# The entry of a two-layer encoder trunk: scale and shift summed on another engine, in pairs, with the loads and transposes in a new order

## The chip, the cores and the metric

The kernel runs on one core of a Trainium2 chip. The metric is device time in microseconds (us) of one execution, as the median of several runs; beside it stands one execution recorded by the hardware profiler. The engines are TensorE (PE: matrix products and transposes, results in PSUM), VectorE (DVE), ScalarE (ACT), GpSimd (POOL) and SyncE (SP, which issues most loads). Each engine works through its own queue in order.

## The reference, cut to what matters

Two layers over a sequence of 1024 tokens with 1024 features, all in float32. Only the first operation of layer 0 is touched by the change:

```
c_act = silu(c)
mod   = c_act @ ada_w[0] + ada_b[0]                  # 1024 x 6144 weights
sh_m, sc_m, g_m, sh_f, sc_f, g_f = split(mod, 6)
h   = rmsnorm(x, norm_g[0, 0]) * (1 + sc_m) + sh_m
bcx = h @ conv_in_w[0]                               # 1024 x 3072: b_gate, c_gate, xh
y   = (b_gate * short_conv(c_gate * xh)) @ conv_out_w[0]
```

Behind it come the rest of layer 0 (norm, MLP of width 4096), a shared key and value side, and layer 1 with latent attention and a second MLP.

## The kernel before, in words

`conv_phase` (L841) is the entry. The eight tiles of x, 128 tokens each (`xt`), are loaded by `load_x` in two halves of 512 tokens and divided by their root mean square in `norm_x`: ScalarE squares a tile and takes the root (`squares`, L269), VectorE inverts it and scales the tile (L964). The features are cut into eight blocks k of 128 columns. For a block and a half, `turn` transposes four 128x128 pieces on TensorE (L899), and `scaled` applies the block's scale and shift: ScalarE writes the result twice (L905), once rounded to the product format (`hi`) and once in full, and VectorE writes the remainder (`lo`, L906). `products` (L924) then multiplies the block with one column group of conv_in_w: three gates, three matmuls each for hi and lo parts, nine matmuls of 512 columns for a block and a half. The weights of a block are loaded and split into the same two parts by `weights` (L913; ScalarE L160, VectorE L161).

The scale and shift of a block come from 2 x 128 columns of `ada_w` with 1024 rows. `ada` loads them (four loads of 256 KB into one of three buffers `aw`), and `ada_end` (L884) multiplies the eight row groups with silu(c), kept in `csil`, and accumulates on VectorE (L887, L889); two float32 matmuls with a column of ones (L891) sum over the partitions, and VectorE adds gain and bias into `sh[k]` (L892, L894).

The loop of L986 goes over k; the second half of x follows the first two blocks behind (`LAG`). The output column group m=0 is finished here; for m=1 the same operands are multiplied again (L1009 on), while VectorE forms the sums that the later groups need (`sums`, L948). `pinned` fixes the order of an engine's queue as written: in this stretch of TensorE and SP; ScalarE and VectorE are ordered by the scheduler of the framework. The gains and biases are loaded as rows on ScalarE's queue at the start (L130 to L139), transposed on TensorE (L864, L867) and copied by VectorE.

Of the kernel before, what the change touches and what calls it, by code (L numbers as in the profile page):

```python
# [36 lines left out]
LAG = 2  # L37
# [12 lines left out]
def trunk_kernel(ctx: ExitStack, tc: tile.TileContext, x, c, ada_w, ada_b, norm_g, conv_in_w, conv_w,  # L50
# [73 lines left out]
    nc.scalar.activation(csil, craw, AF.Exp, scale=-1.0)  # L124
# [3 lines left out]
    vrows, brows = rows_[:, :P], rows_[:, P:2 * P]  # L128
    r = 0
# [8 lines left out]
    nc.scalar.dma_start(brows[0:96, :], ada_b.rearrange("l (k p) -> (l k) p", p=P))  # L138
    nc.scalar.dma_start(brows[96:112, :], kv_ada_b.rearrange("(k p) -> k p", p=P))  # L139
# [23 lines left out]

    nc.vector.tensor_scalar(csil, csil, 1.0, None, op0=ALU.add)
# [676 lines left out]
    def conv_phase():  # L841
# [20 lines left out]

        p_ = tp_ps()
        nc.tensor.transpose(p_[:, :VEC_ROWS], vrows[:VEC_ROWS, :], ident[:VEC_ROWS, :VEC_ROWS])  # L864
        nc.vector.tensor_copy(vecs, p_[:, :VEC_ROWS])
        p_ = tp_ps()
        nc.tensor.transpose(p_[:, :BIAS_ROWS], brows[:BIAS_ROWS, :], ident[:BIAS_ROWS, :BIAS_ROWS])  # L867
        nc.vector.tensor_copy(bias, p_[:, :BIAS_ROWS])
# [15 lines left out]
        def ada_end(k, raw):  # L884
            p_ = tp_ps()
            acc = st.tile([P, 2 * P], F32, tag="av", name=nm("av"), bufs=2)
            nc.vector.tensor_scalar(acc, raw[:, 0, :], csil[:, 0:1], None, op0=ALU.mult)  # L887
            for i in range(1, KD):
                nc.vector.scalar_tensor_tensor(acc, raw[:, i, :], csil[:, i:i + 1], acc, op0=ALU.mult, op1=ALU.add)  # L889
            for j in range(2):  # L890
                nc.tensor.matmul(p_[:, j:j + 1], acc[:, j * P:(j + 1) * P], ones[:, 0:1], start=True, stop=True)  # L891
# [21 lines left out]
        def weights(k, m):  # L913
# [3 lines left out]
               conv_in_w[0][k * P:(k + 1) * P, :].rearrange("p (g c) -> p g c", g=3)[:, :, m * P:(m + 1) * P])  # L917
# [48 lines left out]
        def first_half(k):  # L966
# [4 lines left out]
            elif k == LAG:  # L971
                load_x(1)
# [9 lines left out]
        with pinned([mybir.EngineType.PE, mybir.EngineType.SP]):  # L982
# [3 lines left out]
            for k in range(KD + LAG):  # L986
# [12 lines left out]
                if k == KD:  # L999
                    w.append(weights(0, 1))  # L1000
# [530 lines left out]
```

## Time and profile before

| | |
|---|---|
| median of 3 runs | 2171.38 us (2169.84 to 2172.59) |
| profiled execution | 2170.84 us, span of its records 2169.1 us |
| TensorE busy | 2068.5 us, 95% of the span |
| VectorE, ScalarE busy | 1542.0 us, 1083.7 us |
| mean granted TensorE clock | 0.988 |

The span is the time from the first to the last recorded instruction. Busy times of engines overlap. A granted clock of 1.00 is 2.4 GHz, 0.50 is 1.2 GHz. Times in rows count from the start of the span.

### The profile page before, as it was taken

Reading aid. Unit: us, or ns where it says so; the run is one execution under the profiler, and the core shown is the slowest. Engines: PE = TensorE matmul, PEld = TensorE weight load, DVE = VectorE, ACT = ScalarE, POOL = GpSimd, SP = SyncE. Lnnn points to the kernel's source line nnn. Section 1 sums busy time; section 2 is a strip of 40 time slices with the busy share of each in tenths; the row PEclk is TensorE's granted clock in tenths of the full one; section 3 lists DMA queues with packets and bytes.
Section 4 is the critical chain, followed back from the end, with each engine's and each line's share of the span. In section 5 each row is a group of like instructions: output and inputs, shape, how many; then the busy total and the mean of one; then the engine's idle time right before and its main releaser. Section 6 shows DMA issues by size and latency. Waiting matters only on the chain.

```text
span 2169.1 us, 25064 instructions
## 1 busy us (share of the span) xinstructions
PE 2068.5 (95%) x9438; PEld 1690.3 (78%) x9438; DVE 1542.0 (71%) x2087; ACT 1083.7 (50%) x1533; POOL 5.3 (0%) x13
## 2 busy tenths in 40 slices
PE   4999999889999999998999999989899999999998
PEld 3788878678888788886777888878678888788886
DVE  6877866877655669877688887665876665566576
ACT  4533353735554444455665655564744454544443
POOL 0000000000000000000000000000000000000000
PEclk9999999999999999998999999999999999999999
DMA  7344464256444889546213331043255553774355
GB/s 227 112 140 146 137 200 143 85 195 206 152 146 141 285 289 327 191 152 216 87 50 123 94 104 36 29 156 127 77 194 185 189 170 121 268 247 164 96 174 172
DMA packets 251023, 344.47 MB, mean 159 GB/s; under 512 B 19253, under 2 KB 142482, under 8 KB 250902
## 3 DMA queue, kind: packets, MB, share of 16 engines
q1 hardware_dynamic: 208408, 252.50, 37.0%
q10 hardware_dynamic: 42494, 90.38, 11.2%
q8 instruction: 74, 1.21, 0.2%
q14 instruction: 47, 0.39, 0.1%
HBM read 258.94 MB, written 83.89 MB: 158 GB/s over the span
## 4 chain that ended last, share of the span: by engine, by line
PE 75%; DVE 13%; ACT 6%; DMA 4%; issue 2%; ACTq 0%; SPq 0%; DVEq 0%
PE one L157 41%; PE mm L157 19%; PE tp L157 7%; PE big L157 4%; PE big L1334 2%; ACT junk L272 2%; DMA raw<-in_ada_w_dram 1%; DVE y L328 1%; PE tp L1360 1%; DVE raw L329 1%; DVE acc L187 1%; DMA raw<-ha 1%; DVE av L889 1%; ACT z L1192 1%; DMA aw<-in_ada_w_dram 1%
## 5 line engine op out<-in xcount | busy, mean ns | idle before, releaser
L157 PE MATMUL one<-slot,uphi 128*128 128x512 f32 x1224 | 377.8, 390 | 0.0
L157 PEld LDWEIGHTS one<-slot,uphi 128*128 128x128 f32 x1224 | 230.4, 188 | 48.1 <-issue 0.5
L157 PE MATMUL one<-ring,ring 128*128 128x512 f32 x1152 | 263.0, 390 | 2.3 <-DVE ring L161 2.3
L157 PEld LDWEIGHTS one<-ring,ring 128*128 128x128 f32 x1152 | 215.8, 188 | 48.4 <-ACT ring L160 3.1
L157 PE MATMUL one<-slot,uplo 128*128 128x512 f32 x612 | 240.9, 394 | 8.6 <-DVE y L516 3.8
L161 DVE TENSOR_TENSOR uplo<-raw,uphi 128x1024 fp32r<-128x1024 f32 x127 | 153.2, 1221 | 131.2 <-ACT uphi L160 131.2
L161 DVE TENSOR_TENSOR ring<-raw,ring 128x1024 fp32r<-128x1024 f32 x144 | 174.2, 1219 | 55.8 <-ACT ring L160 55.4
L160 ACT ACTIVATE ring<-raw 128x1024 fp32r<-128x1024 f32 x144 | 149.5, 1051 | 110.6 <-DMA raw<-ha 60.2
L157 PE MATMUL mm<-ring,ring 128*128 128x512 f32 x768 | 189.3, 396 | 7.0 <-DVE ring L161 7.0
L160 ACT ACTIVATE uphi<-raw 128x1024 fp32r<-128x1024 f32 x127 | 134.5, 1060 | 113.0 <-PE one L157 82.1
L157 PE MATMUL big<-slot 128*128 128x512 f32 x768 | 178.9, 393 | 5.3 <-DVE slot L161 4.5
L157 PE MATMUL tp<-ring,ring 128*128 128x512 f32 x768 | 183.9, 389 | 0.0
L160 ACT ACTIVATE ring<-w 128x1024 fp32r<-128x1024 f32 x80 | 84.8, 1060 | 186.0 <-PE tp L157 95.7
L157 PEld LDWEIGHTS mm<-ring,ring 128*128 128x128 f32 x768 | 146.3, 191 | 39.8 <-DVE ring L161 6.0
L157 PEld LDWEIGHTS big<-slot 128*128 128x128 f32 x768 | 144.5, 189 | 36.5 <-DVE slot L161 5.2
L157 PEld LDWEIGHTS tp<-ring,ring 128*128 128x128 f32 x768 | 144.0, 188 | 29.8
L161 DVE TENSOR_TENSOR ring<-w,ring 128x1024 fp32r<-128x1024 f32 x80 | 97.7, 1221 | 88.5 <-ACT ring L160 87.9
L157 PEld LDWEIGHTS one<-slot,uplo 128*128 128x128 f32 x612 | 115.3, 188 | 36.8 <-DVE y L516 5.5
L187 DVE SCALAR_TENSOR_TENSOR acc<-raw,csil,acc 128x1024 f32<-128x1024 f32 x88 | 112.5, 1279 | 27.6 <-DMA raw<-in_ada_w_dram 23.1
L514 ACT ACTIVATE y<-one 128x512 f32<-128x512 f32 x66 | 39.0, 592 | 165.0 <-PE one L157 111.3
L157 PE MATMUL mm<-slot,uphi 128*128 128x512 f32 x344 | 108.7, 398 | 9.5 <-DVE slot L386 9.3
L157 PE MATMUL one<-slot,s 128*128 128x512 f32 x468 | 114.5, 394 | 3.3 <-DVE s L161 3.3
(268 smaller groups left out, 3464.9 us busy)
## 6 DMA issues: line engine op xcount, KB each, us to landing
ha<-y ACTq DMA_DIRECT2D x224, 256.0 KB, 4.1
raw<-ha SPq DMA_DIRECT2D x112, 512.0 KB, 4.0
raw<-in_ada_w_dram SPq DMA_DIRECT2D x80, 512.0 KB, 4.0
raw<-in_mlp_up_w_dram SPq DMA_DIRECT2D x70, 512.0 KB, 4.2
w<-in_mlp_down_w_dram SPq DMA_DIRECT2D x48, 512.0 KB, 6.8
raw<-in_mlp_down_w_dram SPq DMA_DIRECT2D x32, 512.0 KB, 4.7
raw<-in_conv_in_w_dram SPq DMA_DIRECT2D x18, 512.0 KB, 4.0
xs<-raw ACTq DMA_DIRECT2D x18, 512.0 KB, 2.6
```

Of the source, the lines that this page charges most:

```text
L157: nc.tensor.matmul(out_, lhs[a], rhs[b], start=first and i == 0, stop=last and i == 2, skip_group_check=more)
L160: nc.scalar.activation(hi, src, AF.Copy)
L161: nc.vector.tensor_tensor(lo, src, hi.bitcast(F32), op=ALU.subtract)
L187: nc.vector.scalar_tensor_tensor(acc, raw, s, acc, op0=ALU.mult, op1=ALU.add)
L272: nc.scalar.activation(junk, src, AF.Square, accum_out=ss)
L328: nc.vector.scalar_tensor_tensor(y, y, rroot(ss), self.gmb, op0=ALU.mult, op1=ALU.mult)
L329: nc.vector.tensor_tensor(xr, xr, y, op=ALU.add)
L514: nc.scalar.activation(dst, x_, AF.Copy)
L889: nc.vector.scalar_tensor_tensor(acc, raw[:, i, :], csil[:, i:i + 1], acc, op0=ALU.mult, op1=ALU.add)
L1192: nc.scalar.activation(y[32 * i:32 * i + 32, :], p_[32 * j:32 * j + 32, :], AF.Copy, scale=scale)
L1334: nc.tensor.matmul(o_, a, m_, start=j == 0, stop=j == 4)
L1360: nc.tensor.transpose(p_[:, c:c + P], pts[4 * hf + i][:, j * P:(j + 1) * P], ident)
```

## The change

Scale and shift of blocks 0 and 1 are summed wholly on TensorE: 16 matmuls with the weights as the stationary operand and a column of `csil` as the moving one (`ada_one`). Blocks 2 to 7 are taken in pairs: one load buffer of twice the width (`aw2`, three of them), one accumulation on VectorE over 512 columns for two blocks (`ada_sum`), and the sums over partitions as before (`ada_two`). The first half of x is loaded ahead of everything else on SP's queue, and the loads of all blocks are issued in one row. In the loop the transposes and the scaling of a block and half stand one step ahead of the products, and two steps of the next pair's accumulation are written into each step. The order of ScalarE and VectorE is fixed as written as well. On ScalarE's queue the bias rows are loaded ahead of the other vectors, and two small activations (`warm`) call for the function tables of Exp and Sqrt.

```diff
     ld(craw, c.rearrange("o (k p) -> p (o k)", p=P))
-    nc.scalar.activation(csil, craw, AF.Exp, scale=-1.0)
     nc.scalar.dma_start(cs, consts[:, :C_T])
...
+    nc.scalar.dma_start(brows[0:96, :], ada_b.rearrange("l (k p) -> (l k) p", p=P))
+    nc.scalar.dma_start(brows[96:112, :], kv_ada_b.rearrange("(k p) -> k p", p=P))
...
+    warm = small()
+    nc.scalar.activation(warm, eps_1, AF.Exp)
+    nc.scalar.activation(csil, craw, AF.Exp, scale=-1.0)
+    nc.scalar.activation(warm, eps_1, AF.Sqrt)
...
+        load_x(0)
...
-        def ada(k):
+        def ada(k, n=1):
-            raw = st.tile([P, KD, 2 * P], F32, tag="aw", name=nm("aw"), bufs=3)
+            raw = st.tile([P, KD, 2, n * P], F32, tag=f"aw{n}", name=nm("aw"), bufs=2 if n == 1 else 3)
             for i in (0, 4):
                 for j, col in enumerate((D, 0)):
-                    ld(raw[:, i:i + 4, j * P:(j + 1) * P],
-                       w0[i * P:(i + 4) * P, col + k * P:col + (k + 1) * P].rearrange("(k p) m -> p k m", p=P))
+                    ld(raw[:, i:i + 4, j, :],
+                       w0[i * P:(i + 4) * P, col + k * P:col + (k + n) * P].rearrange("(k p) m -> p k m", p=P))
...
+        def ada_one(k, raw):
+            p_ = tp_ps()
+            for j in range(2):
+                for i in range(KD):
+                    nc.tensor.matmul(p_[:, j:j + 1], raw[:, i, j, :], csil[:, i:i + 1], start=i == 0, stop=i == KD - 1)
+            ada_end(k, p_)
+
+        def ada_sum(raw):
+            acc = st.tile([P, 2, 2 * P], F32, tag="av", name=nm("av"), bufs=2)
+
+            def step(i):
+                if i == 0:
+                    nc.vector.tensor_scalar(acc, raw[:, 0], csil[:, 0:1], None, op0=ALU.mult)
+                else:
+                    nc.vector.scalar_tensor_tensor(acc, raw[:, i], csil[:, i:i + 1], acc, op0=ALU.mult, op1=ALU.add)
+
+            return acc, [lambda i=i: step(i) for i in range(KD)]
+
+        def ada_two(k, acc):
+            for i in range(2):
+                p_ = tp_ps()
+                for j in range(2):
+                    nc.tensor.matmul(p_[:, j:j + 1], acc[:, j, i * P:(i + 1) * P], ones[:, 0:1], start=True, stop=True)
+                ada_end(k + i, p_)
...
         with pinned([mybir.EngineType.PE, mybir.EngineType.SP]):
...
+            raws, ws = [ada(0)], [load_weights(0, 0)]
+            load_x(1)
+            raws.append(ada(1))
+            ws.append(load_weights(1, 0))
+            raws += [ada(k, 2) for k in (2, 4, 6)]
             acc = banks6()
...
+            with pinned([mybir.EngineType.Activation, mybir.EngineType.DVE]):
+                norm_x(0)
+                w.append(split_weights(ws[0]))
+                ada_one(0, raws[0])
+                scaled(0, turn(0, 0), *place(0, 0))
+                products(w[0], 0, 0, acc)
+                norm_x(1)
+                w.append(split_weights(ws[1]))
+                ada_one(1, raws[1])
+                scaled(1, turn(1, 0), *place(1, 0))
+                scaled(0, turn(0, 1), *place(0, 1))
+                products(w[1], 1, 0, acc)
+                scaled(1, turn(1, 1), *place(1, 1))
+                products(w[0], 0, 1, acc)
+                av, steps = ada_sum(raws[2])
+                for step in steps:
+                    step()
+                ws = [load_weights(k, 0) for k in (2, 3)]
+                before = 1, 1
+                for k in range(2, KD, 2):
+                    w += [split_weights(q) for q in ws]
+                    ada_two(k, av)
+                    more = k + 2 < KD
+                    if more:
+                        av, steps = ada_sum(raws[k // 2 + 2])
+                    ws = [load_weights(k + i, 0) for i in (2, 3)] if more else [load_weights(0, 1)]
+                    for i in range(k, k + 2):
+                        for half in range(2):
+                            scaled(i, turn(i, half), *place(i, half))
+                            if more:
+                                steps.pop(0)()
+                                steps.pop(0)()
+                            products(w[before[0]], *before, acc)
+                            before = i, half
+                products(w[before[0]], *before, acc)
+            w = split_weights(ws[0])
```

## Rows read from the trace of the kernel before

**Rows 1.** Stretches: us, busy PE, PEld, DVE, ACT, POOL, clock, DMA share, GB/s

```profile
0.00:86.35 86.35, 54.95 (x243) 42.97 (x244) 57.82 (x142) 45.25 (x77) 1.48 (x9) 0.94 0.62 176
...
86.35:119.00 32.65, 32.65 (x146) 27.03 (x145) 28.73 (x43) 15.60 (x27) 0.96 (x1) 1.00 0.58 178
```

**Rows 2.** Chain that ended last, in order of time: start, us, what

```profile
29.09 4.85 DMA aw<-in_ada_w_dram
...
84.37 2.13 PE one L157 x8
```

**Rows 3.** Groups of VectorE, 0 to 86.35 us: busy us, mean ns, idle before

```profile
L889 DVE SCALAR_TENSOR_TENSOR av<-aw,csil,av 128x256 f32<-128x256 f32 x56 | 26.6, 481 | 1.4 <-DMA aw<-in_ada_w_dram 0.5
L161 DVE TENSOR_TENSOR w<-w,w 128x384 fp32r<-128x384 f32 x11 | 6.1, 553 | 1.8 <-ACT w L160 1.8
L964 DVE TENSOR_SCALAR y<-y,small 128x1024 f32<-128x1024 f32 x8 | 6.0, 750 | 0.1
...
L892 DVE SCALAR_TENSOR_TENSOR sh<-tp,g,b 128x1 f32<-128x1 f32 x8 | 1.7, 217 | 5.0 <-PE tp L891 5.0
```

**Rows 4.** One line later in the kernel (L1183): duration min/median/max in ns

```profile
L1183 DVE SCALAR_TENSOR_TENSOR lat<-lat,vecs,sq x8: 737/744/752, 1075.3 to 1131.2; 128x512 f32<-128x512 f32 x8
```

**Rows 5.** Timeline of TensorE: start, us, instruction, what it waited for

```profile
39.84 0.99 PE L891 MATMUL tp<-ones,av 128*128 128x1 f32 x4 [6.90 <-DVE av L889]
40.69 2.91 PE L157 MATMUL mm<-slot,w 128*128 128x512 f32 x6
...
62.22 0.58 PE L891 MATMUL tp<-ones,av 128*128 128x1 f32 x4 [0.39 <-DVE av L889]
62.65 1.63 PE L157 MATMUL mm<-slot,w 128*128 128x512 f32 x6
...
78.56 0.60 PE L899 MATMUL tp<-cs,y 128*128 128x128 f32 x4
...
81.08 0.60 PE L899 MATMUL tp<-cs,y 128*128 128x128 f32 x4
```

**Rows 6.** Stretches, as rows 1, for the loads

```profile
0.00:9.50 9.50, 0.00 (x0) 0.00 (x0) 2.74 (x11) 2.01 (x3) 1.48 (x9) 1.00 0.78 209
10.50:13.50 3.00, 0.83 (x2) 0.36 (x2) 1.56 (x7) 2.88 (x5) 0.00 (x0) 1.00 1.01 385
...
28.50:34.50 6.00, 4.44 (x23) 3.55 (x21) 3.70 (x12) 4.92 (x10) 0.00 (x0) 1.00 1.21 291
```

**Rows 7.** Stretches, as rows 1, for the clock

```profile
36.50:43.50 7.00, 3.66 (x11) 3.11 (x12) 6.05 (x16) 1.45 (x2) 0.00 (x0) 0.51 0.56 152
...
45.50:48.00 2.50, 0.88 (x3) 0.52 (x4) 2.43 (x6) 2.07 (x4) 0.00 (x0) 1.00 0.00 0
68.50:70.00 1.50, 0.20 (x2) 0.23 (x3) 1.50 (x4) 0.04 (x1) 0.00 (x0) 1.00 0.00 0
71.00:74.00 3.00, 3.00 (x9) 2.22 (x9) 0.69 (x1) 1.25 (x2) 0.00 (x0) 0.50 0.23 66
```

**Rows 8.** Timeline of the start: start, us, instruction

```profile
6.75 0.32 ACTq L139 DMA_DIRECT2D raw<-in_kv_ada_b_dram  x1
...
10.59 1.06 ACT L272 ACTIVATE junk<-y 128x1024 bf16<-128x1024 f32 x1 [2.94 <-DMA y<-in_x_dram]
...
12.23 0.42 PE L867 MATMUL tp<-cs,raw 112*128 112x112 f32 x1 [0.92 <-DMA raw<-in_kv_ada_b_dram]
...
13.25 1.04 ACT L272 ACTIVATE junk<-y 128x1024 bf16<-128x1024 f32 x1
...
14.62 1.04 ACT L272 ACTIVATE junk<-y 128x1024 bf16<-128x1024 f32 x1
```

**Rows 9.** Groups of ScalarE, 0 to 86.35 us, as rows 3

```profile
L905 ACT ACTIVATE slot<-tp,sh 128x512 fp32r<-128x512 f32 x12 | 9.3, 778 | 23.4 <-DVE sh L894 19.4 <-PE tp L899 2.9 <-DVE small L279 1.0
...
L160 ACT ACTIVATE w<-w 128x384 fp32r<-128x384 f32 x11 | 5.7, 520 | 7.5 <-PE one L157 2.8 <-DMA w<-in_conv_in_w_dram 2.1 <-DMA aw<-in_ada_w_dram 1.9
...
L124 ACT ACT_TABLE_LOAD x1 | 1.3, 1283 | 3.7 <-DMA cs<-in_consts_dram 3.7
```

More of the change, by code (lines that the diff above doesn't have):

```diff
@@ L36 @@
 AHEAD = 4
-LAG = 2
 PAIRS = D_FF // P // 2
@@ L861, in load_x @@
                 ld(xt[t], x0[t * P:(t + 1) * P, :])
+        load_x(0)
+        p_ = tp_ps()
+        nc.tensor.transpose(p_[:, :BIAS_ROWS], brows[:BIAS_ROWS, :], ident[:BIAS_ROWS, :BIAS_ROWS])
+        nc.vector.tensor_copy(bias, p_[:, :BIAS_ROWS])
         p_ = tp_ps()
@@ L873, in conv_phase, with ada_end @@
         sh = [cp.tile([P, 2], F32, name=nm("sh")) for _ in range(KD)]
-        def ada(k):
-            raw = st.tile([P, KD, 2 * P], F32, tag="aw", name=nm("aw"), bufs=3)
+        def ada(k, n=1):
+            raw = st.tile([P, KD, 2, n * P], F32, tag=f"aw{n}", name=nm("aw"), bufs=2 if n == 1 else 3)
             for i in (0, 4):
                 for j, col in enumerate((D, 0)):
-                    ld(raw[:, i:i + 4, j * P:(j + 1) * P],
-                       w0[i * P:(i + 4) * P, col + k * P:col + (k + 1) * P].rearrange("(k p) m -> p k m", p=P))
-            return raw
[L884 to L891, printed above, removed]
+                    ld(raw[:, i:i + 4, j, :],
+                       w0[i * P:(i + 4) * P, col + k * P:col + (k + n) * P].rearrange("(k p) m -> p k m", p=P))
+            return raw
+        def ada_end(k, p_):
             nc.vector.scalar_tensor_tensor(sh[k][:, 0:1], p_[:, 0:1], g1[:, k:k + 1], b1[:, k:k + 1], op0=ALU.mult,
@@ L911, in conv_phase, with load_weights @@
         new = [None] * 4
-        def weights(k, m):
+        def load_weights(k, m):
             raw = ad.tile([P, D], F32, tag=("acc", "gmb")[k % 2], name=nm("w"), bufs=1)[:, :3 * P]
@@ L920, in weights @@
             return w
+        def weights(k, m):
+            return split_weights(load_weights(k, m))
         late = []
@@ L964, in norm_x, with place @@
                 nc.vector.tensor_scalar(xt[t], xt[t], rroot(squares(nx, xt[t])), None, op0=ALU.mult)
-        def first_half(k):
-            raw = ada(k)
-            if k == 0:
-                load_x(0)
-                norm_x(0)
-            elif k == LAG:
-                load_x(1)
-            p_ = turn(k, 0)
-            ada_end(k, raw)
-            scaled(k, p_, old(k), ("11", "21")[k // 4])
-        def second_half(k):
+        def place(k, half):
+            if not half:
+                return old(k), ("11", "21")[k // 4]
@@ L978, in second_half @@
             if k < 4:
                 new[k] = halves(raw_tile())
-            scaled(k, turn(k, 1), new[k % 4][k // 4], ("12", "22")[k // 4])
+            return new[k % 4][k // 4], ("12", "22")[k // 4]
         with pinned([mybir.EngineType.PE, mybir.EngineType.SP]):
-            w = [weights(0, 0)]
-            first_half(0)
-            acc = banks6()
-            for k in range(KD + LAG):
-                if k < KD - 1:
-                    w.append(weights(k + 1, 0))
-                    first_half(k + 1)
-                if k < KD:
-                    products(w[k], k, 0, acc)
-                if k == LAG:
-                    norm_x(1)
-                    second_half(0)
-                if k >= LAG:
-                    if k - LAG < KD - 1:
-                        second_half(k - LAG + 1)
-                    products(w[k - LAG], k - LAG, 1, acc)
-                if k == KD:
-                    w.append(weights(0, 1))
```

10 lines of the change are left out of this document (4 added, 6 removed).

## Prediction

> **What bounds the kernel now.** I read three views for the first 119 us, the only part that the change touches: the stretches, the chain that ended last, and the timeline. The stretches [rows 1] show two regimes. Up to 86.35 us the matrix engine (TensorE, PE) is busy 55.0 us of 86.35 and starved for the rest; from there it is busy 32.65 of 32.65 us. The boundary is the end of the products of block column m=0: the chain puts the last eight of them at 84.37 to 86.5 us [rows 2], and the 144 products of m=1 then run without a pause, 0.227 us each [rows 1]. What follows is set by TensorE, so a microsecond gained or lost before 86.35 should reach the end nearly whole. In the starved part the chain alternates between VectorE's accumulation (`ada_end`) and loads of the modulation weights that are issued late because their three buffers are still in use; one such row stands for three [rows 2]. So I need one number: E, the time at which the products of m=0 end in the changed kernel, against 86.35.
>
> **What is removed.** Eight accumulations leave VectorE: each seven instructions of 0.481 us plus a first one [rows 3], about 3.8 us, 30 us in all. In come three accumulations over pairs, eight instructions of 512 elements each. The nearest row of that shape took 0.744 us [rows 4]; with a hand-over of 0.04 us, an estimate, I take 0.78, so 6.2 us a pair and 18.7 in all. Blocks 0 and 1 go to TensorE: 16 calls with one column each. The trace records four instructions for two such calls, 0.43 us at the full clock (62.22 to 62.65) and 0.85 us from 39.84 to 40.69, when the granted clock was 0.50, the 1.2 GHz level [rows 5, 7]. A block is 32 instructions: 3.4 us or 6.8 us. VectorE saves 11 us, but that is worth something only where it is what TensorE waits for, so I follow the new order.
>
> **Term 1, the load queue.** All loads of the entry are now issued in one go on SP's queue, in this order: half of x (2.10 MB), block 0 and its product weights (1.05 + 0.20), the other half of x (2.10), block 1 with its weights (1.25), three pairs (6.29), and only then the product weights of blocks 2 and 3 (0.39). No buffer wait holds any of it. Rates: rows of x in 4 KB pieces moved at 385 GB/s, modulation weights in 512 B pieces at 290 [rows 6]. From a start at about 2.2 us (at these rates the 1.99 MB of the first 9.5 us [rows 6] take some 7): x with 0.19 MB of small vectors 6.0, to 8.2; block 0 4.3, to 12.5; x 5.4, to 17.9; block 1 4.3, to 22.2. The pairs come in 1 KB pieces, which no row shows: between 16.3 us (385) and 21.7 us (290). A cost per piece plus one per byte fitted through the two rows puts 1 KB near 345 GB/s, an estimate; I take 18.2 us, to 40.4. Blocks 2 and 3's product weights add 1.4, to 41.8. Those 1.99 MB end just past the first x tile (the 1.95th MB), whose reader started at 10.59 [rows 8]: 1.1 us to land. So the last of them is there at **42.9**, bounds 41.0 and 46.4.
>
> The Trainium skill ("DMA: Bandwidth & Descriptors", Specifications) states that pieces of 512 B and more reach the line rate. By it the wider pieces of a pair gain nothing over single ones. By it the weights land at 46.4, by the fit at 42.9. The trace disagrees with it for single pieces, 290 against 385 GB/s [rows 6]; no row shows the doubled ones.
>
> On VectorE the splits of these two weights stand ahead of `ada_end`, so blocks 2 and 3 wait for them: ScalarE's copy 0.52, VectorE's remainder 0.55, then 0.22 for the scale and about as much for the shift [rows 3, 9]; with hand-overs 1.5 us. The transposes of block 2 start at **G = 44.4** by this path.
>
> **Term 2, the engines' own path to G.** ScalarE's queue: its nine loads ended at 7.07 with 1.5 us of table load and Exp between them [rows 8, 9], so 5.6 without; then two table loads of 1.28 and three small instructions, 8.9. The table loads now precede x instead of following it, which is the saving of `warm`. Four squares at a pitch of 1.37 (13.25 to 14.62 [rows 8]) and the last scaling 0.75 [rows 3]: half of x is ready at 15.5. TensorE meanwhile sums block 0 from about 11.5 (the last small vector, issued 1.5 us earlier than in the kernel before, was transposed there at 12.23 [rows 8]; the loads of block 0 land by 13.6) to between 16.5 and 18.3. Scaling, then ScalarE turns to the other half of x (5.5 us): 26 to 27. Block 1's sums on TensorE stand behind the products of block 0 and end between 25.5 (full clock) and 31 (half). Then two halves scaled (four passes of 0.78 [rows 9], which overlap to some 0.68 each), the remainders, products, the last transposes of block 1 and its remainder: 34 to 38. Only then, in VectorE's fixed order, the pair sum of blocks 2 and 3: 6.2. Then 1.1 for the splits and 0.4: G = 41.7 to 46. Both paths end close together; the queue's 44.4 is the middle, and I take it. It means TensorE stands idle from about 34 to 44 except for 0.8 us of sums, where the kernel before had 6.9 us of idle time at 33 to 40 and then ran until 43.5 at clock 0.50, 3.7 us [rows 5, 7]. I charge the same here: 1.9 us.
>
> **Term 3, after G.** A step is four transposes and nine products: 78.56 to 81.08, 2.52 us [rows 5]. Twelve steps, 30.2; the last nine products 2.04. VectorE needs about 0.7 for the remainder (also 512 elements from two operands, as in [rows 4]) and 1.56 for two sum steps per step, 2.3 against 2.52, so within a pair TensorE sets the pace and "a step ahead" hides ScalarE's passes. At the two borders between pairs it does not: from the start of a pair's last transposes, 0.6 for them, 1.35 for ScalarE's two passes, 0.7 and 1.56 on VectorE, then TensorE's eight one-column instructions, the splits ahead of `ada_end` (1.1) and `ada_end`: 5.65 us until the next transposes, where a step alone is 2.52. So 3.1 more per border, 6.2 for two, of which some 2.3 each are idle time of TensorE. Sum: 30.2 + 2.0 + 6.2 + 1.9 = 40.4, E = 84.8. Idle stretches of that length cost the clock in one case (after 68.4 to 70.2 the clock was 0.50 from 71 to 74) and not in another (45.6 to 48) [rows 7]. With two of them I charge one drop, half of just over 3 us, 1.6: **E = 86.4**, +0.1 us; bounds none and 3.2.
>
> **Smaller parts.** Bias and vector loads change places on ScalarE's queue, covered by the x loads; uncovered it would be a microsecond at the start, and the start has 2 us of slack against the queue. Product weights from block 4 on wait for the splits two blocks back and then have a whole pair, 13 us, to land. The sums of m=1 can no longer begin early (5 us of VectorE work moved behind E): VectorE was busy 28.7 of 32.65 us there, part of it filler needed much later [rows 1]; I take nothing.
>
> **Rivals.**
> *Faster.* The pairs move as x does. Then the weights land at 41.0 and G is 42.5 at a start in full clock; TensorE's idle stretch shrinks and the clock survives it and the borders: 42.5 + 38.5 = 81.0, -5.3 us, **2165.5**. For it: the pieces are twice as long and x reached 385. Against it: the engines' own path must run at its quick end too.
> *Slower.* The product weights of blocks 2 and 3 stand behind 6.3 MB, and those move no faster than the 512 B pieces. At 290 GB/s G = 47.9 and E = 89.9, +3.5; at 265 GB/s +5.5, **2176.4**. It decides from 280 GB/s down, where it passes 4.3 us. For it: the trace's longest 512 B stretch ran at 290 [rows 6]. Against it: the pieces are wider.
> By the skill's rule named above the pairs would run at the 512 B rate: **2174.4**, which is this rival short of its point; as far as the rows bear it out, 1 in 10, counted with the unchanged cases.
> *The sums on TensorE are the new wait.* At half clock both blocks cost 13.6 us and G is 46: E = 88.0, +1.6, **2172.5**. For it: after a pause the same instructions ran at half pace in the row at 39.84 [rows 5]; against it: the first pauses of TensorE in the changed kernel are short, and the queue ends 1.6 us before this path even then.
>
> **How the numbers follow.** The profiled execution took 2170.84 us with a span of 2169.1, and the median of three runs is 2171.38, 0.5 above; the sum is made against 2170.84. +0.1 gives **2171.0**. Chances: my forecast 0.36, the sums on TensorE 0.15, the rule's case 0.10, together 0.61 within 0.2% (4.3 us, about what a measurement of this kernel can tell from no change); faster 0.22; slower 0.17. The range reaches to the faster rival and to the slower one at 265 GB/s: **2165.5 to 2176.5**.
>
> **What would show it.** Right: SP's issues without long pauses to about 40 us, the first copy of product weights for block 2 or 3 waiting for a load at 41 to 46 us, VectorE's accumulation down to some 19 us, transposes of block 2 at 42 to 48 us, two pauses of TensorE of about 2 us before the sums of blocks 4 and 6, and the last product of m=0 at 82 to 91 us. Wrong: if the weights of blocks 2 and 3 land well before the pair sum ends, term 1 falls; if TensorE keeps the full clock from 12 us to the end, my clock charges of 3.5 us fall; if TensorE pauses within m=1, the carry falls.

## The result, and the profile after

The changed kernel took 2180.84 us in the median of 20 runs (2173.83 to 2188.88), the kernel before 2169.61 (2167.91 to 2178.45): ratio 1.0044, interval 1.0034 to 1.0054. It is slower by some 10 us, and above the predicted range of 2165.5 to 2176.5. The first profiled execution was one of the quickest, 2175.47 us with a span of 2173.5; a further one, taken as an experiment (e14_again), took 2180.85 us, the median, with a span of 2177.8. Both are read here, since they differ in one thing, the time that block 1's sums took, and what stands behind these sums up to E differs with it.

Stretches of the first trace, columns as in [rows 1]:

```profile
0.00:86.35 86.35, 62.22 (x284) 51.41 (x285) 43.28 (x92) 40.88 (x71) 1.48 (x9) 0.90 0.58 176
86.35:119.00 32.65, 32.65 (x144) 26.69 (x144) 30.29 (x48) 16.51 (x29) 0.95 (x1) 1.00 0.45 131
6.00:7.00 1.00, 0.29 (x1) 0.02 (x1) 0.28 (x1) 0.98 (x1) 0.00 (x0) 1.00 0.62 125
8.00:10.00 2.00, 0.41 (x1) 0.18 (x1) 0.70 (x5) 1.99 (x4) 0.00 (x0) 1.00 0.81 182
...
26.00:42.00 16.00, 13.83 (x65) 10.91 (x64) 6.38 (x14) 6.69 (x13) 0.00 (x0) 0.79 1.09 348
```

Up to 86.35 us VectorE has 14.5 us less work (43.3 against 57.8 [rows 1]), yet TensorE is not through sooner. The wide pieces of the pairs move at 348 GB/s, against 291 and 385 in [rows 6]. Groups of VectorE, up to 90 us, beside [rows 3]:

```profile
L906 DVE SCALAR_TENSOR_TENSOR av<-aw,csil,av 128x512 f32<-128x512 f32 x21 | 15.8, 750 | 0.5
...
L904 DVE TENSOR_SCALAR av<-aw,csil 128x512 f32<-128x512 f32 x3 | 1.4, 481 | 0.0
```

Timeline of TensorE, columns as in [rows 5]; L896 is a block's one-column sums, L914 those of a pair, L920 transposes, L155 products. First trace:

```profile
13.24 6.97 PE L896 MATMUL tp<-csil,aw 128*128 128x1 f32 x32 [4.18 <-DMA aw<-in_ada_w_dram]
...
23.43 2.50 PE L155 MATMUL mm<-slot,w 128*128 128x512 f32 x5 [0.61 <-DVE slot L927]
...
27.00 3.99 PE L896 MATMUL tp<-csil,aw 128*128 128x1 f32 x32
...
46.62 1.84 PE L914 MATMUL tp<-ones,av 128*128 128x1 f32 x8 [6.17 <-DVE av L906]
48.32 1.09 PE L920 MATMUL tp<-cs,y 128*128 128x128 f32 x4
```

The same instructions in the execution of 2180.85 us:

```profile
13.94 6.96 PE L896 MATMUL tp<-csil,aw 128*128 128x1 f32 x32 [4.09 <-DMA aw<-in_ada_w_dram]
...
27.71 6.82 PE L896 MATMUL tp<-csil,aw 128*128 128x1 f32 x32
...
50.65 1.84 PE L914 MATMUL tp<-ones,av 128*128 128x1 f32 x8 [5.79 <-DVE av L906]
52.35 1.09 PE L920 MATMUL tp<-cs,y 128*128 128x128 f32 x4
...
94.37 1.53 PE L155 MATMUL mm<-slot,w 128*128 128x512 f32 x6
```

Block 0's sums run at 0.21 us an instruction in both; block 1's at 0.12 in one and 0.21 in the other. What is behind them moves with them: G, the start of block 2's transposes, is 48.32 or 52.35 (forecast 44.4), and E, the end of m=0, 89.88 or 94.37 against 86.35 [rows 1]. E is 3.5 and 8.0 us later than before, and the span ends 4.4 and 8.7 us later: what is late at E stays late in these two.

The chain of waits of the slower execution shows what holds block 2 (start, us, what):

```profile
27.91 6.62 PE tp L896 x32
...
40.25 1.28 PE one L155 x3
41.53 0.87 PE tp L920 x4
42.42 0.78 ACT b L926
43.20 0.68 ACT raw L926
45.03 0.76 DVE av L906
...
49.75 0.76 DVE av L906
50.65 1.84 PE tp L914 x8
```

The pair sum of blocks 2 and 3 stands on VectorE behind the last remainder of block 1. That remainder needs everything that TensorE did at half pace. The product weights, my forecast's bound, were not the last here: ScalarE's copy of them ran at 46.70, the pair sum ended at 50.4. In the first trace the copy ran at 45.92 and the pair sum ended at 46.47. Timeline of ScalarE, first trace, then the median execution:

```profile
45.92 1.12 ACT L158 ACTIVATE w<-w 128x384 fp32r<-128x384 f32 x2 [6.08 <-DMA w<-in_conv_in_w_dram]
...
46.70 1.13 ACT L158 ACTIVATE w<-w 128x384 fp32r<-128x384 f32 x2 [2.83 <-DMA w<-in_conv_in_w_dram]
```

### The profile page after: what moved, and what is told of

Its sections match the earlier page's. It is cut to its first block, busy times and chain, and to the rows that moved or that the text cites. A ratio compares the mean times of both kernels' runs of the same rounds, so it can differ in the third digit from the quotient of the medians.

```text
span 2173.5 us, 25102 instructions
## 1 busy us (share of the span) xinstructions
PE 2078.9 (96%) x9494; PEld 1702.3 (78%) x9494; DVE 1533.4 (71%) x2047; ACT 1083.3 (50%) x1535; POOL 5.3 (0%) x13
## 3 DMA queue, kind: packets, MB, share of 16 engines
q10 hardware_dynamic: 42494, 90.38, 11.2%
## 4 chain that ended last, share of the span: by engine, by line
PE 77%; DVE 12%; ACT 6%; DMA 3%; issue 2%; ACTq 0%; SPq 0%; DVEq 0%
PE one L155 42%; PE mm L155 19%; PE tp L155 6%; PE big L155 5%; PE big L1376 2%; ACT junk L274 2%; DVE y L330 1%; DMA raw<-in_ada_w_dram 1%; PE tp L1402 1%; DVE raw L331 1%; DMA raw<-ha 1%; DVE acc L189 1%; DVE ring L159 1%; ACT z L1234 1%; DVE pt L1406 1%
## 5 line engine op out<-in xcount | busy, mean ns | idle before, releaser
L155 PE MATMUL one<-slot,uphi 128*128 128x512 f32 x1224 | 378.6, 390 | 0.0
L155 PEld LDWEIGHTS one<-slot,uphi 128*128 128x128 f32 x1224 | 231.0, 189 | 48.3 <-issue 0.5
L155 PE MATMUL one<-ring,ring 128*128 128x512 f32 x1152 | 263.0, 390 | 2.3 <-DVE ring L159 2.3
L155 PEld LDWEIGHTS one<-ring,ring 128*128 128x128 f32 x1152 | 215.9, 188 | 48.3 <-ACT ring L158 3.1
L155 PE MATMUL one<-slot,uplo 128*128 128x512 f32 x612 | 241.2, 394 | 8.2 <-DVE y L518 3.8
L155 PE MATMUL mm<-ring,ring 128*128 128x512 f32 x768 | 187.9, 394 | 9.8 <-DVE ring L159 9.8
L155 PE MATMUL tp<-ring,ring 128*128 128x512 f32 x768 | 183.9, 389 | 0.0
L155 PE MATMUL big<-slot 128*128 128x512 f32 x768 | 179.3, 394 | 4.5 <-DVE slot L159 4.5
L155 PEld LDWEIGHTS mm<-ring,ring 128*128 128x128 f32 x768 | 145.2, 190 | 42.3 <-DVE ring L159 6.7
L155 PEld LDWEIGHTS big<-slot 128*128 128x128 f32 x768 | 145.3, 190 | 35.4 <-DVE slot L159 5.2
L155 PEld LDWEIGHTS tp<-ring,ring 128*128 128x128 f32 x768 | 144.0, 188 | 29.8
L155 PEld LDWEIGHTS one<-slot,uplo 128*128 128x128 f32 x612 | 115.4, 189 | 36.0 <-DVE y L518 5.5
L155 PE MATMUL one<-slot,s 128*128 128x512 f32 x468 | 114.5, 394 | 4.0 <-DVE s L159 4.0
L155 PE MATMUL mm<-slot,uphi 128*128 128x512 f32 x344 | 108.2, 396 | 9.5 <-DVE slot L388 9.3
```

Source lines behind the costliest of these rows:

```text
L155: nc.tensor.matmul(out_, lhs[a], rhs[b], start=first and i == 0, stop=last and i == 2, skip_group_check=more)
```

## The experiments

G and E are those of the profiled execution, medians those of all runs; the kernel before, on the same chips, had medians of 2169.6 to 2171.5.

| kernel | G, us | E, us | median, us | 95% interval of the ratio to before |
|---|---|---|---|---|
| changed, first trace | 48.32 | 89.88 | 2180.84 | 1.0034 to 1.0054 |
| e14_again (one run) | 52.35 | 94.37 | 2180.85 | |
| e1_again | 48.27 | 91.12 | 2179.99 | 1.0034 to 1.0060 |
| e2_weights_early | 48.63 | 90.10 | 2178.38 | 1.0028 to 1.0054 |
| e3_sum_early | 46.97 | 88.64 | 2175.06 | 1.0013 to 1.0042 |
| e4_both | 42.75 | 85.90 | 2170.04 | 0.9992 to 1.0010 |
| e5_warm | 44.15 | 85.82 | 2171.21 | 1.0000 to 1.0020 |
| e6_border | 45.90 | 89.71 | 2174.19 | 1.0011 to 1.0029 |
| e7_sums_dve | 48.01 | 91.19 | 2175.35 | 1.0017 to 1.0036 |
| e9_steps_first | 45.65 | 82.14 | 2167.81 | 0.9979 to 0.9997 |
| e10_split_sum | 46.42 | 82.76 | 2170.03 | 0.9987 to 1.0004 |
| e11_wide_wait | 48.30 | 90.05 | 2178.08 | 1.0025 to 1.0049 |
| e12_wide_sums | 44.36 | 80.81 | 2167.14 | 0.9976 to 0.9994 |
| e13_wide_warm | 41.16 | 77.68 | 2164.71 | 0.9967 to 0.9985 |
| e15_after_wide | 48.25 | 91.22 | 2176.37 | 1.0019 to 1.0041 |

### Queue or pair sum: e1 to e4

e1_again is the changed kernel again.

> The changed kernel as it is, profiled a second time, because the runs of it spread over 15 us (2174 to 2189) and the first profile is one of its quickest executions, with 3.5 us lost by the end of the products of m=0. Theory A, the loss is all in the entry and its size varies there: the median stays 9 to 12 us above the kernel before, and the second profile ends m=0 at 90 to 101 us, later by as much as its own time is longer, with nothing added after it. Rival B, the rest is lost behind the entry: m=0 ends near 90 us again and the difference grows afterwards.

e2_weights_early:

```diff
-            raws += [ada(k, 2) for k in (2, 4, 6)]
+            raws.append(ada(2, 2))
+            ws23 = [load_weights(k, 0) for k in (2, 3)]
+            raws += [ada(k, 2) for k in (4, 6)]
```

> Only the loads of the product weights of blocks 2 and 3 are moved, from behind the three pairs to behind the first. In the profile of the changed kernel these weights reach ScalarE at 45.9 us, and the pair sum of blocks 2 and 3 ends on VectorE at 46.5. Theory A, both hold back block 2 alike: under 1 us faster than the changed kernel, m=0 ends at 89 to 90 us in an execution like the first. Rival B, the load queue alone holds it back: 4 to 7 us faster.

e3_sum_early:

```diff
+                av, steps = ada_sum(raws[2])
+                for step in steps[:2]:
+                    step()
                 scaled(1, turn(1, 0), *place(1, 0))
                 scaled(0, turn(0, 1), *place(0, 1))
+                for step in steps[2:]:
+                    step()
```

> Only the pair sum of blocks 2 and 3 is moved on VectorE, from behind the last remainder of block 1 into its idle time before (two of eight steps ahead of the first remainder of block 1, six behind the second half of block 0); it should end at about 40 us. Theory A, the weights hold block 2 back as well: within 1 us of the changed kernel. Rival C, the engines' own path alone holds it back: 4 to 7 us faster.

e4_both has both edits.

> Both moves of the two kernels before it. Theory A: the transposes of block 2 start at 41 to 43 us in place of 48.1, TensorE's idle time of 6.2 us shrinks to under 1 and the clock does not fall there, so m=0 ends 6.5 to 9 us sooner, at about 82 us, and the time is 6 to 9 us below the changed kernel in a like execution. If B or C is right, no more than the better one of the two single moves.

e1_again came out as its theory A has it: 9.9 us above the kernel before, E at 91.12. Measured against it, on one chip: the weights alone 1.6 us (inside the spread of the runs), the pair sum alone 4.9, both 10.0. ScalarE's copy of the weights ran at 40.05 in e2_weights_early, and G stayed at 48.63 since the pair sum still ended at 46.9 (theory A). In e3_sum_early the pair sum was through at 40, and G moved only to 46.97, because the copy then waited for its load (timeline of ScalarE):

```profile
45.02 1.11 ACT L158 ACTIVATE w<-w 128x384 fp32r<-128x384 f32 x2 [5.63 <-DMA w<-in_conv_in_w_dram]
```

By its trace, with block 1's sums quick (3.89 us), that is theory A; the 4.9 us of the median are what rival C forecast. Both fit what the two traces of the changed kernel show: in the quick one the two waits end within 0.6 us of each other; in the median execution the pair sum ends 3.7 us after the copy began, so that moving the sum alone wins until the copy bounds block 2. So two waits hold block 2, and each can hide the other. With both gone the loss is gone; block 2 then starts with a short pause (timeline of TensorE, e4_both):

```profile
42.75 0.66 PE L920 MATMUL tp<-cs,y 128*128 128x128 f32 x4 [0.62 <-DVE sh L890]
```

E was 85.90 there and not about 82 as theory A of e4_both has it: the pace was lost at both borders between pairs (nine products in 4.19 and 3.79 us).

### Who sums blocks 0 and 1: e7

```diff
         def ada_one(k, raw):
             p_ = tp_ps()
+            av1 = st.tile([P, 2, 2 * P], F32, tag="av", name=nm("av"), bufs=2)[:, :, :P]
+            nc.vector.tensor_scalar(av1, raw[:, 0], csil[:, 0:1], None, op0=ALU.mult)
+            for i in range(1, KD):
+                nc.vector.scalar_tensor_tensor(av1, raw[:, i], csil[:, i:i + 1], av1, op0=ALU.mult, op1=ALU.add)
             for j in range(2):
-                for i in range(KD):
-                    nc.tensor.matmul(p_[:, j:j + 1], raw[:, i, j, :], csil[:, i:i + 1], start=i == 0, stop=i == KD - 1)
+                nc.tensor.matmul(p_[:, j:j + 1], av1[:, j, :], ones[:, 0:1], start=True, stop=True)
             ada_end(k, p_)
```

> e4_both with scale and shift of blocks 0 and 1 accumulated on VectorE again (eight instructions of 256 elements and two one-column products for each block), in the same place of the order. Theory A (the sums on TensorE save VectorE time, and that is worth something for block 1 alone, whose sums stand right behind the second half of x): block 0's scale is there at about 20.5 us (21.4 in e4_both), block 1's 2.6 us later, the pair sum of blocks 2 and 3 by 2.5 to 3.8 us later; m=0 ends at 88.5 to 90, about 2173. Theory B (the one-column sums cost as much on TensorE, and drop its clock): m=0 within 1 us of 86.1, about 2170. Theory C (TensorE, idle for longer, stays at half clock for longer): m=0 past 90, over 2174.

2175.35 against 2170.04 for e4_both, on another chip (against the kernel before 1.0026 and 1.0001): with all else alike, moving these sums to TensorE is worth some 5 us, half pace included. E at 91.19 and the time are in theory C's range, and its mechanism shows: after a wait of 12.15 us for block 0's sums TensorE left half pace for the first time at 44.24 us, in e4_both at 27.79 (the first rise in each trace's clock records). How much of the 5 us is VectorE's time and how much TensorE's pace isn't told apart. Block 0's scale was no sooner either (its transposes at 22.52, in e4_both at 21.19). In the order of e4_both, this part of the change is not what lost the time.

### TensorE's pace: e5, e11, e12, e13, e15

e5_warm (on e4_both):

```diff
+                p_ = tp_ps()
+                for _ in range(16):
+                    nc.tensor.matmul(p_[:, :P], ones, ones, start=True, stop=True)
                 ada_one(0, raws[0])
```

> e4_both with 16 extra products of 128 columns on TensorE (ones by ones, result not used) ahead of block 0's one-column sums, in the stretch in which TensorE waits for that block's load (9.5 to 14.4 us of e4_both). Theory A (the half clock at the start is what makes the sums of block 0 cost 6.96 us; wide products raise it, and the engines' path, not the queue, now sets the transposes of block 2): the 32 sums take 3.5 to 4.0 us, block 2 starts up to 3.4 us before 42.75, and m=0 ends at 82.5 to 84.5: about 2167. Theory B (the one-column sums run at half clock whatever stands ahead of them): the sums still take about 7 us, m=0 ends at 86, about 2170. Theory C (the sums do run at full clock, but the second half of x or a load sets what follows): sums 3.5 us, m=0 at 85.5 to 86, about 2170.

No theory held (E is the one that C forecast, by another way). Block 0's sums took 4.61 us, quick at first; then the granted clock fell to 0.50, the 1.2 GHz level, at 17 us while TensorE ran these one-column instructions back to back, and stayed there to 41. Block 1's sums took 6.82 us. What was won at the first block was lost at the second. Stretch of e5_warm, columns as in [rows 1]:

```profile
17.00:37.00 20.00, 17.91 (x68) 15.23 (x68) 8.08 (x19) 10.10 (x20) 0.00 (x0) 0.50 1.10 340
```

e11_wide_wait is the changed kernel with 24 such products ahead of `ada_two` of blocks 2 and 3.

> The changed kernel with 24 extra products of 128 columns (ones by ones, result not used; 4.6 us at the full clock) on TensorE in its wait for the pair sum of blocks 2 and 3 (40.4 to 46.6 us). Theory A (that pause costs the clock: the products of the first step behind it run at half pace until 51 us, 1.5 to 3 us): the granted clock stays at 1.00 over 41 to 52 us, m=0 ends 1.5 to 3 us sooner than 89.9 to 91.3, and the time is 2177 to 2178 in the median where the changed kernel had 2180 to 2181. Theory B (the clock falls for another reason, one-column sums among them, whatever TensorE does in the pause): 0.5 to 0.6 for 44 to 51 us as before, time 2180 to 2181. Theory C (the extra products end after the pair sum and delay the sums): block 2's transposes past 49 us, time 2181 to 2183.

The extra products took 5.52 us where 4.6 was expected. The clock stayed at 1.00 over the pause and the products behind it took 2.33 us for nine instead of 3.52. The median of five runs is 2 to 3 us lower, with an interval that overlaps the changed kernel's. But the pace was then lost at the next border (nine products in 3.47 at 61.77), so the profiled E gained nothing: theory A for the pause, not for the sum.

e12_wide_sums (on e9_steps_first, below):

```diff
-            for j in range(2):
-                for i in range(KD):
-                    nc.tensor.matmul(p_[:, j:j + 1], raw[:, i, j, :], csil[:, i:i + 1], start=i == 0, stop=i == KD - 1)
+            for i in range(KD):
+                nc.tensor.matmul(p_[0:1, :2 * P], csil[:, i:i + 1], raw[:, i].rearrange("p a b -> p (a b)"),
+                                 start=i == 0, stop=i == KD - 1)
+            row = st.tile([P, 2, 2 * P], F32, tag="av", name=nm("av"), bufs=2)[0:1, 0, :]
+            nc.vector.tensor_copy(row, p_[0:1, :2 * P])
+            p_ = tp_ps()
+            for j in range(2):
+                nc.tensor.matmul(p_[:, j:j + 1], row[:, j * P:(j + 1) * P], ones[0:1, 0:1], start=True, stop=True)
             ada_end(k, p_)
```

> e9_steps_first with the sums of blocks 0 and 1 on TensorE the other way round: a column of csil is the stationary operand and the 256 weights of a row group are the moving one, eight instructions of 256 columns that leave a row, which VectorE copies and two small products turn into columns. Theory A (the one-column form doesn't raise TensorE's pace, the wide one does): block 0's sums start at half pace and speed up, or the products behind them run at 0.23 us instead of 0.50; block 1's sums take 3.4 to 4 us instead of 6.82; block 2's transposes come at 38 to 42 us instead of 45.65, m=0 ends at 75 to 79, and the time falls by 2 to 5 us, to 2163 to 2166. Theory B (the pace depends on something else than the form): block 1's sums 6.8 us plus 0.7 for the turn, 2168 to 2169. Theory C (the wide form costs more columns than it saves, 0.43 us each at the full clock): sums of 4.5 us and more, no gain.

e13_wide_warm has the 16 products of e5_warm as well.

> e12_wide_sums with the 16 extra products of 128 columns of e5_warm ahead of block 0's sums. In e5_warm these raised the pace (the first one-column sums ran in 0.12 us) and it fell again 2.4 us into the sums. Theory A (wide sums hold the pace that wide products have raised): both blocks' sums in 3.4 to 4 us each, block 0's scale at 18.5 to 19.5, block 2's transposes at 35 to 39 and m=0 at 72 to 76: 2160 to 2164. Theory B (it falls again whatever the form): no better than e12_wide_sums. Theory C (a load or the second half of x sets block 2): both speed up and m=0 ends no sooner than in e12_wide_sums.

Timeline of TensorE in e13_wide_warm (L895 the wide sums, L1020 the extra products):

```profile
9.52 5.88 PE L1020 MATMUL tp<-ones 128*128 128x128 f32 x32
15.33 3.61 PE L895 MATMUL tp<-aw,csil 128*1 128x256 f32 x16
...
22.90 1.43 PE L155 MATMUL mm<-slot,w 128*128 128x512 f32 x5 [0.89 <-DVE slot L932]
...
25.53 4.63 PE L895 MATMUL tp<-aw,csil 128*1 128x256 f32 x16
...
41.16 0.66 PE L925 MATMUL tp<-cs,y 128*128 128x128 f32 x4
```

The wide sums held the pace that the extra products had raised: 3.61 us for block 0, and the five products at 22.90 took 1.43 us instead of 2.50. Block 1's took 4.63 and 4.58 us in the two kernels. The granted clock still fell twice, near 24 and 34 us, each time behind waits of 0.4 to 0.9 us. G and E gain 4.5 us from e9_steps_first to e13_wide_warm, the median 3.1; e12_wide_sums alone gains 1.3 us in E, and its median (0.7) is inside the spread. So theory A of e13_wide_warm came true for block 0 alone: G, E and the median lie 2.2, 1.7 and 0.7 us past its ranges. Theory A of e12_wide_sums missed all the times that it gave; block 1's 4.58 us are what theory C forecast, though E did gain. In e12_wide_sums block 0's wide sums took 6.54 us, and the transposes behind them 0.66, where they take 1.09 behind the one-column sums: the wide form brought TensorE to its full pace, which five products in 2.50 us at 25.07 then show lost again.

e15_after_wide puts the two edits of e13_wide_warm into the changed kernel and nothing else.

> The changed kernel with the wide form of block 0's and 1's sums and the 16 extra products ahead of them (the two edits of e13_wide_warm), and nothing else: load order, pair sum and borders stay as the change has them. Theory A (the half pace makes block 1 late, and the pair sum in its fixed place behind block 1 carries that to block 2): block 1's sums end near 31 instead of 34.5, the pair sum at 44 to 46.5 instead of 50.4, block 2's transposes then wait for the product weights on the queue (45.9 in the first trace of the changed kernel) and start at 47.5 to 48.5 instead of 52.35; m=0 ends at 88 to 90, and the median is 2174 to 2176.5 instead of 2180.8. Theory B (the pace isn't what makes the typical execution late): 2179 to 2181. Theory C (the two other bounds are met earlier than that, so the pace is worth all of the loss): under 2172.

2176.37, 4.5 us below the changed kernel and on another chip. Against the kernel before beside each, the loss went from 11.2 to 4.9 us by the medians, and from 1.0044 to 1.0030 by the ratios, with intervals that overlap: the pace alone is worth some 3 to 6 us of the loss. The two traces of the changed kernel differ by 4.5 us at E. The pair sum now ended at 46.3, and the weights were copied at 46.28: the other two bounds are met there, as theory A says. E at 91.22 is past its range, as the pace was lost at the second border (nine products in 4.19 us).

### The borders between pairs: e6, e9, e10

e6_border (on e4_both) writes the next pair's accumulation as 3, 3 and 2 steps and takes `ada_two` ahead of the fourth step of a pair.

> e4_both with the accumulation of the next pair written as 3, 3 and 2 steps into the first three of the four steps of a pair, and its one-column sums with scale and shift ahead of the fourth, so that no pair waits for the accumulation at its start. Theory A (a border costs 3.1 us and, by its pause, a stretch at half clock): two borders less the 1.0 us of one-column sums that stay, 2 x 2.1 to 2 x 2.6, and 3 to 5 us of half clock: m=0 ends at 77 to 80 instead of 86.1, and the time falls by 6 to 9 us, to 2161 to 2164. Theory B (VectorE, with 0.7 us for a remainder and 2.3 us for three steps in a step of 2.52 us, becomes the bound): m=0 ends at 83 to 85, 2167 to 2169. Theory C (what is won before the end of m=0 isn't carried, as VectorE is late with the sums of the next columns): m=0 ends early, and the time stays within 2 us of 2170.

No theory held: the pauses became longer (2.10 us for 1.72), and this execution had block 1's sums at 6.82 us, so G was 3.2 us late besides. The last accumulation steps still stood behind a remainder, which waits for ScalarE's two passes.

e9_steps_first (on e4_both):

```diff
-                    w += [split_weights(q) for q in ws]
                     ada_two(k, av)
+                    w += [split_weights(q) for q in ws]
...
-                            scaled(i, turn(i, half), *place(i, half))
-                            if more:
+                            if more and (i, half) != (k, 0):
+                                steps.pop(0)()
+                                steps.pop(0)()
+                            scaled(i, turn(i, half), *place(i, half))
+                            if more and (i, half) == (k, 0):
                                 steps.pop(0)()
                                 steps.pop(0)()
```

> e4_both with another order on VectorE: in the second, third and fourth step of a pair the two accumulation steps for the next pair stand ahead of the remainder, not behind it, and at a border the one-column sums and scale and shift stand ahead of the splits of the product weights. e6_border, with three steps to a slot, still paused 2.10 us at each border, because the last accumulation steps stood behind a remainder that waits for ScalarE's two passes. Theory A (that order, not the amount of work, makes the border): the pauses of 1.72 us go to 0.6 or less, TensorE keeps the full clock over the borders, and from block 2's transposes to the end of m=0 it takes 35 to 38 us instead of 43.3: with the transposes at 42.8 to 45.9 (as the clock falls at block 1's sums) m=0 ends at 78 to 84, and the time is 2162 to 2167. Theory B (VectorE has 10.9 us of work in a pair of 11.1 us and becomes the bound, so small pauses come in every step): 40 us and more, 2167 to 2169. Theory C (what is won before the end of m=0 isn't carried): m=0 ends early, time within 2 us of 2170.

From G to E it took 36.5 us instead of 43.2, and TensorE had no pause at a border; pauses of 0.37 to 0.55 us inside the pairs were all that VectorE's load cost. Theory A held but for the time, 0.8 us past its range. E came 4.2 us before that of the kernel before; of this 1.5 was left at the end of the profiled span. In e13_wide_warm 6.9 of 8.7 us were left. Which later wait took the rest wasn't traced.

e10_split_sum (on e9_steps_first) sums block 0's scale on TensorE and accumulates its shift on VectorE.

> e9_steps_first with block 0's scale summed on TensorE (16 instructions of one column) and its shift accumulated on VectorE (eight instructions of 128 elements and one product), which in e4_both was idle from 15.9 to 21.3 us while TensorE worked at the sums. Theory A (the sums of block 0 set what follows up to block 2): the scale is there at 18.5 to 19.5 us instead of 21.4, block 2's transposes and the end of m=0 come 2 to 3 us sooner than in e9_steps_first, and so does the time. Theory B (the second half of x sets what follows: its squares on ScalarE end late anyway): under 0.7 us. Theory C (fewer instructions on TensorE, a longer pause, a later rise to the full clock): no gain or a loss of up to 3 us.

The scale was summed by 17.4 us, but TensorE took the shift's product only at 20.99: VectorE, which first scales x, had it no sooner. No gain; a slower bound took the place. The median is 2.2 us above that of e9_steps_first, as theory C allows; E is 0.6 later.

### Is a delay of the entry carried: e8

```diff
             acc = banks6()
+            for _ in range(18):
+                nc.tensor.matmul(acc[1, 0], w[0][:, :P], ops["11"][0][0], start=True, stop=True)
             for k in range(KD):
```

> The kernel before with 18 extra products of 512 columns at the full clock between the last product of m=0 and the first of m=1, written into a bank that the next product clears: all that follows is 18 x 0.227 = 4.1 us later and nothing else differs. Theory A (a delay of the entry is carried as it is, and no more): 2170 + 4.1 = 2174 us, interval 1.0013 to 1.0025. Theory B (the last 140 us, in the second MLP, lose a further 4 us in most executions when they come some us later, as in part of the executions of the changed kernel): 2176 to 2180. Theory C (later waits absorb part of a delay): 2171 to 2173.

2174.41 us (7 runs), ratio 1.0026, interval 1.0016 to 1.0037: 3.5 to 8.0 us for 4.1 put in. The delay is carried (theory A). Two of the seven took 2177.6 and 2178.9; whether they lost more in the last stage, as theory B has it, isn't known, as the profiled one did not. That such a loss exists, two other traces show (under e14 below).

### The median execution: e14

> The changed kernel once more, unchanged, for the trace of another execution; the profiled ones so far took 2175.5 and 2177.8 us, while 26 executions had a median near 2181. Theory A (the alternation of block 1's sums makes most executions slow): if this one takes 2179 us or more, its block 1 sums take 6.8 us, the pair sum of blocks 2 and 3 ends near 49.5 instead of 46.5, and m=0 ends at 92 to 94. Theory B (the loss is in the last 140 us): block 1's sums 3.9 us, m=0 at 90 to 91.5, and from the last copy of the scores to the end 145 us instead of 141. If it takes under 2178 us, it tells them apart only by which of the two it doesn't show.

Theory A: block 1's sums 6.82 us, the pair sum to 50.4, E at 94.37. From the last copy that the expectation means (a copy in the second MLP, L680, at 2035.9) to the end it took 141.9 us, as in the kernel before (141.0), so this execution did not lose in the last stage. Others do. Stretches from behind that copy to the end, e14_again, then e4_both (its copy at 2028.9):

```profile
2036.50:2177.80 141.30, 130.52 (x574) 107.10 (x572) 92.71 (x95) 54.53 (x68) 0.00 (x0) 0.98 0.44 153
...
2029.50:2174.20 144.70, 133.43 (x574) 109.17 (x572) 92.74 (x95) 54.53 (x68) 0.00 (x0) 0.95 0.43 150
```

In the profiled executions of e2_weights_early and e4_both it took 145.1 and 145.3 us from the copy on, with TensorE's granted clock at 0.95 in that stretch where it was 0.98; in the 15 other traces 140.3 to 142.5. So there is a second source of some 4 us, far behind the entry, and a time near 2181 can come about in two ways. That a typical execution is one with slow sums rests on one trace and on e15_after_wide, which takes the half pace away and has its median where the quick executions are.

## Why the prediction was wrong

**The carry, and term 3, were right for these executions.** From G to E I forecast 40.4 + 1.6 = 42.0 us; the two traces have 41.6 and 42.0. A step took 2.52 us, each border paused 1.72 us where 2.3 was reckoned, and the clock was lost behind G and at one border, as reckoned. So nearly the whole miss is in G: 52.35 in the median execution where I took 44.4, 7.95 us. The rest of the miss of 9.85, 1.9, is about 0.7 lost between E and the end, and 1.3 outside the span (3.05 us where the profiled run before had 1.74).

**Term 1, half right.** The guessed rate of 1 KB pieces, 345 GB/s, measured 348. The prediction's fit through the two rows comes to 338 and 18.6 us for the pairs, not to 345 and 18.2, so the closer agreement is luck. The queue as a whole was 3 to 4 us late (45.9 and 46.7 against 42.9): x and the first blocks did not keep 385 and 290 GB/s through the first 10 us (125 GB/s at 6 to 7 us, 182 at 8 to 10). At 6 to 7 us ScalarE's small vectors moved as well, at 8 to 10 none of them did; what held the queue there isn't shown. The Trainium skill ("DMA: Bandwidth & Descriptors", Specifications) has pieces of 512 B and more at line rate; by these rows 512 B, 1 KB and 4 KB stand at 291, 348 and 385, so the size still matters above that. The rival with the queue as bound therefore holds only in the quick executions, and there for a late start instead of a low rate.

**Term 2 failed, and it decides.** I put the end of block 1's last remainder at 34 to 38 us. It was 40.5 in the first trace and 44.5 in the median execution, and the pair sum behind it took the 6 us that I had given it. Of the 6.5 us past 38, 3.4 had gathered when block 1's sums ended (34.4 against my latest 31), and 3.1 came behind them. The working charged half pace to the one-column sums alone, and only as an upper end; the products and transposes between them were taken at the full clock. The clock column, from which [rows 7] are taken, doesn't show this so early: in the kernel before, the stretch 24.98 to 29.00 reads 1.00, while six products took 2.91 us there, 0.48 each, and 0.227 is the full clock [rows 1]. The trace holds records of the granted clock only from its first rise to 1.00 on, at 29.85 us in the kernel before, and where it holds none the column reads 1.00. Stretch and timeline of TensorE, kernel before:

```profile
24.98:29.00 4.02, 4.02 (x11) 3.04 (x12) 3.73 (x11) 3.43 (x6) 0.00 (x0) 1.00 1.09 359
...
24.98 2.91 PE L157 MATMUL mm<-slot,w 128*128 128x512 f32 x6
```

That row stood in the trace I had. It says that TensorE had not left half pace at 25 us. The Trainium skill ("TensorE: Matmul & The Clock Gate", Part 1: The HAM clock gate) calls the throttled state the default, released by activity; the trace agrees, with 0.48 to 0.50 us a product up to 27 us in both kernels. My rival "the sums on TensorE are the new wait" had the mechanism with G at 46 and 2172.5 us. Its size was wrong by 6.4 us: sums that began at 13.9 instead of 11.5 since they waited for their load (which the prediction itself had landing by 13.6), and half pace over all of TensorE's work on blocks 0 and 1.

**The tie that I split.** I saw both paths end within a few us and took the queue's 44.4, which lay in the middle of the engines' 41.7 to 46. With two paths of uncertain length the later one sets the end, so the time to expect lies above the later of the two middles; e2 to e4 show both paths there.

**Why a quick entry is not a fast kernel.** The savings came true: half of x was ready at 15.6 (forecast 15.5) and VectorE's accumulation fell to 17.2 us. They did not shorten the wait that counted, as a 6 us pair sum was put, in a fixed order, where TensorE waits for it: 6.17 us in the first trace, 6.90 for the accumulation there before [rows 5]. In e9_steps_first and e13_wide_warm, with that sum moved, the entry ends sooner than before.

## What to carry to other kernels

Where an order is fixed by hand, ask of each long instruction sequence what stands ahead of it in its queue and how late that can be; an accumulation whose data is there goes into the idle time ahead of such a wait, not behind it. Two waits that end together hide each other, so an experiment has to take away both. At a kernel's start take TensorE's pace from the duration of its instructions, as the clock column reads 1.00 where the trace holds no record.

## What the runs showed of the hardware

The column of the granted clock showed 1.00 while instructions ran at half pace: over 21 to 43 us of the median execution (below). In e9_steps_first it reads 1.00 from the start to the end of m=0, though block 1's sums took 6.82 us.

```profile
21.00:43.00 22.00, 19.91 (x68) 16.29 (x68) 6.73 (x16) 10.56 (x20) 0.00 (x0) 1.00 1.11 338
```

The two are not at odds. The first clock record of each trace is a rise to 1.00: at 29.85 us in the kernel before, 27.76 in the first trace, 43.12 in the median execution, 42.76 in e9_steps_first. Before it instructions run at half pace, the 1.2 GHz level, and behind it at full pace; the column's 1.00 ahead of it stands for no record.

Instructions of one column left TensorE at half pace although it was busy with them for 7 us, and in e5_warm the granted clock fell to 0.50 amid them. The same sums with 256 moving columns, behind the same extra products, ran in 3.61 us. In the kernels with block 1's one-column sums these took 3.8 to 4.1 us in six profiled executions and 6.8 in five, one and the same kernel showing both. In the six the first rise came at 26.7 to 28.5 us, about when these sums began; without extra products the four slow ones had it at 42.8 to 44.2. What decides between the two isn't shown. This makes a part of the spread of several us between executions of the changed kernel; the last stage can make another.
